# A gated delta rule whose scan applies raw keys and then the triangular inverse, in a two-layer hybrid trunk

## The chip, the cores and the metric

The kernel runs on one NeuronCore of one Trainium2 chip. The metric is the device time of an execution in microseconds (us). TensorE (PE) multiplies matrices into PSUM; VectorE (DVE), ScalarE (ACT) and GpSimd (POOL) work on SBUF tiles, and DVE and ACT read PSUM too; SyncE (SP) issues most of the DMA transfers. Each engine runs its own instructions in order and waits on semaphores for the others.

## What is computed

A trunk of two layers on 1024 tokens of width 1024: chunked attention with an MLP, then gated DeltaNet with an MLP, and a last norm. The change lies in DeltaNet, 8 heads of width 128. Per head, with queries `q` and keys `k` scaled to unit norm, `beta` a gate and `g` a log-decay, the reference does for chunks of 64 tokens:

```
gc = jnp.cumsum(g, axis=-1)
kb = k * beta[..., None];  vb = v * beta[..., None]
L = jnp.where(strict, jnp.einsum('bhnid,bhnjd->bhnij', kb, k) * decay, 0.0)
M = L + jnp.eye(CHUNK)
rhs = jnp.concatenate([vb, kb * jnp.exp(gc)[..., None]], axis=-1)
sol = lax.linalg.triangular_solve(M, rhs, left_side=True, lower=True, unit_diagonal=True)
u, w = sol[..., :dv], sol[..., dv:]
def step(state, inp):
    v_new = u_c - jnp.einsum('bhck,bhkv->bhcv', w_c, state)
    o_c = jnp.einsum('bhck,bhkv->bhcv', qd_c, state) + jnp.einsum('bhij,bhjv->bhiv', qk_c, v_new)
    state = state * gl_c[..., None, None] + jnp.einsum('bhck,bhcv->bhkv', kd_c, v_new)
    return state, o_c
```

`qk` holds the decayed products of queries and keys, `qd` the queries times exp(gc), `kd` the keys times exp(gc_last - gc), and `gl` the decay of a whole chunk. All is f32.

## The kernel before, in words

**Stages.** In the profiled execution attention takes until about 490 us, block 0 (output projection and MLP) until about 1198, DeltaNet until about 1804, and block 1 the rest. Dense products split each f32 operand into a high and a low part and take three products.

**DeltaNet's dense work.** `dn_run` (about L1835) goes through the projection's panels: keys of all heads, then queries, values and z (the output gate) of each head. A panel is 48 matmuls of 128x512: two halves of the tokens, eight slices of the width, three products. In the profile they are `acc<-xs,whi` and `acc<-xs,wlo`.

**What stands between.** After every dense matmul `dn_run` calls `turn`, which lets each task that is ready take a step. Tasks are generators with a priority from the table `G` (scans 0 and 0.1, solves 0.5, inverses 2, blocks 3, keys and values 4, queries 5, outputs 7, weights 8). A task waits for a mark of another one (`until`), for some planned time (`sleep`) or for a tile of a ring (`take`, `give`). A clock of planned costs decides what counts as ready. The order that comes of it is fixed when the program is built, for PE, DVE, ACT and POOL; SP's order is made by the framework's scheduler. Every operation of a task goes through one helper, so the profile shows it at line L163.

**The tasks of a head h.** The work is in blocks of 128 tokens, eight a head.

- `dn_inverses` (L2279 and on) builds the inverse of M for the eight blocks in the tile Zh, which starts at zero and of which there are two; head h waits for the values of head h-2.
- `dn_prep_keys` (L2374 to L2404): a DMA (L2379) loads the raw keys of the head into `kn`, width across partitions, 128 rows of 4 KB. PE transposes four blocks at a time into a PSUM tile (`tp<-ident,kn`), and DVE makes two scaled copies: `kbg` (beta, exp(gc) and the norm `rk`) and `kd`.
- `dn_prep_queries` (L2406 to L2445): `l2_sums` (L2155 to L2171) squares the queries qT on ACT into `nt` and sums over the width with eight one-column multiplies by ones on PE (`tp<-ones,nt`). The row of scales is broadcast by DMA (L1902), the decay `dc` loaded (L2412). PE forms qT·kn (`tp<-qT,kn`), DVE multiplies it by dc into `qk`, and POOL writes the scaled queries into the second half of `WQ`, a tile [128, 8, 2, 128] with two buffers.
- `dn_prep_values` (L2447 to L2488): transposes v, DVE scales it to `vb`; then, for each half of the blocks, PE forms Z·vb (`tp<-vb,Zh`) which ACT copies back to vb (this is u), and kbg·Z (`tp<-Zh,kbg`), which ACT copies into the first half of WQ (this is w).
- `dn_scans` (L2490 to L2535), two tasks, for even and odd heads. A step p multiplies the state by both halves of WQ (`s<-st,WQ`), DVE subtracts (vn = u - w·state), PE forms kd·vn and adds qk·vn to the output in PSUM, DVE updates the state (`st<-st,gl,s`), ACT copies the output block to `o`. The even heads' PSUM tiles appear as `s`, those of the odd heads as parts of `zz`.
- `dn_outs` squares, normalizes and gates o; `dn_reload` brings it back as the operand of the output projection.

Of the kernel before, what the change touches and what calls it, by code (L numbers as in the profile page):

```python
# [7 lines left out]
F32 = mybir.dt.float32  # L8
# [226 lines left out]
class Trunk:  # L235
# [1668 lines left out]
    def dn_gates(self):  # L1904
# [16 lines left out]
        for n in range(2):  # L1921
# [7 lines left out]
        yield  # L1929
        abd = self.abd  # L1930

        room = [self.whole(t).rearrange("p (n t) -> p n t", t=P) for t in ("kn", "qT")]
        used = []

        def t64(name):
# [219 lines left out]
    def l2_sums(self, x, scale, v):  # L2155

        nc = self.nc
        squares = yield from self.take("nt", 2)
        for h in range(2):
            nc.scalar.activation(squares[h], x[:, h * HB : (h + 1) * HB], AF.Square)  # L2160
            yield
        ps = yield from self.take("tp")
        for n in range(8):
            c = slice(n % 4 * P, (n % 4 + 1) * P)
            nc.tensor.matmul(ps[:, n : n + 1], squares[n // 4][:, c], self.ones, start=True, stop=True)
        self.give("nt", *squares)
        yield

        nc.vector.tensor_scalar(v, ps[:, :8], EPS, scale, ALU.add, ALU.mult)
        self.give("tp", ps)  # L2170
        yield  # L2171

    def rsqrt_few(self, v, n, who):
# [105 lines left out]
    def dn_inverse(self, h):  # L2279

        nc, db = self.nc, self.db
        Z = self.Zh[h % 2]
        X = self.X[:, :, 0:32]
        U12 = self.dq.tile([P, 8, 32], F32, name=self.nm("ua"), tag="ua")
        U34 = self.dq.tile([P, 8, 64], F32, name=self.nm("ub"), tag="ub")
# [8 lines left out]
            nc.gpsimd.tensor_tensor(U12[r], U12[r], wide(self.rk[r, h], 32, 32), ALU.mult)  # L2294
        nc.gpsimd.tensor_tensor(U34[0:64], U34[0:64], wide(self.rk[0:64, h], 64, 64), ALU.mult)
        yield from self.until("solve", h // 4)
        if h >= 2:
            yield from self.until("values", h - 2)
        zd, xd = self.solved[h // 4]
        for b in range(4):  # L2300
            r = slice(b * 32 + (h % 4) * 8, b * 32 + (h % 4) * 8 + 8)
# [72 lines left out]
    def dn_prep_keys(self):  # L2374

        nc, db, cols = self.nc, self.db, self.cols
        for h in range(8):
            kn = self.heads["kn", h] = self.whole("kn")
            nc.sync.dma_start(kn, self.kd[h])  # L2379
            self.mark("kn", h)  # L2380
            yield from self.until("rk", h // 4)
            ck = self.sm.tile([P, 2, 8], F32, name=self.nm("ck"), tag="ck")
            for n in range(2):
                nc.vector.tensor_tensor(ck[:, n], cols[:, 2 + n, h], self.rk[:, h], ALU.mult)
            if h == 0:
                yield from self.until("solve", 0)
            yield from self.sleep(G["sl_keys"])
            if h:
                yield from self.until("values", h - 1)
            if h >= 2:  # L2390
                yield from self.until("scan", h - 2)
            kbg = self.dq.tile([P, 8, P], F32, name=self.nm("kbg"), tag="kbg")
            kd = db.tile([P, 8, P], F32, name=self.nm("kd"), tag="kd")
            for q in range(2):
                s = slice(4 * q, 4 * q + 4)
                tp, ps = yield from self.to_tokens(kn, q)
                for n, dst in enumerate((kbg, kd)):
                    nc.vector.tensor_tensor(dst[:, s], ps, wide(ck[:, n, s], P, P), ALU.mult)
                    if n:
                        self.give("tp", tp)  # L2400
                    yield
            self.heads["kk", h] = kbg, kd
            self.mark("keys", h)
            yield from self.until("queries", h)  # L2404

    def dn_prep_queries(self):  # L2406
        nc, db = self.nc, self.db
        for h in range(8):
            yield from self.until("q", h)
            qT = self.heads.pop(("q", h))  # L2410
            dc = self.whole("dc").rearrange("p (q t) -> p q t", t=P)
            nc.sync.dma_start(dc, self.decay[h])  # L2412
            if h == 0:
                yield from self.until("u", 6)
# [10 lines left out]
            kn = self.heads["kn", h]  # L2425
            if h >= 2:
                yield from self.until("scan", h - 2)
            qk = self.qks[h % 2]
            for q in range(2):
                s = slice(4 * q, 4 * q + 4)  # L2430
                tp = yield from self.take("tp")
                ps = tp.rearrange("p (q t) -> p q t", t=P)
                for t in range(4):
                    c = slice((4 * q + t) * P, (4 * q + t + 1) * P)
                    nc.tensor.matmul(ps[:, t], kn[:, c], qT[:, c], start=True, stop=True)
# [4 lines left out]
            WQ = db.tile([P, 8, 2, P], F32, name=self.nm("WQ"), tag="WQ")  # L2440
            nc.gpsimd.tensor_tensor(
                WQ[:, :, 1], qT.rearrange("p (q t) -> p q t", t=P), row.rearrange("p (q t) -> p q t", t=P), ALU.mult)
            self.heads["qq", h] = WQ, qk
            self.mark("queries", h)
            self.mark("q", "used", h)  # L2445
            yield

    def dn_prep_values(self):
        nc, db = self.nc, self.db
        for h in range(8):  # L2450
            yield from self.until("v", h)
            cols = self.cols
            vT, Z = self.heads.pop(("v", h)), self.Zh[h % 2]
# [12 lines left out]
            kbg, kd = self.heads.pop(("kk", h))  # L2466
            WQ, qk = self.heads.pop(("qq", h))
            for q in range(2):
                s = slice(4 * q, 4 * q + 4)
                tp = yield from self.take("tp")  # L2470
                ps = tp.rearrange("p (q t) -> p q t", t=P)
                for t in range(4):
                    nc.tensor.matmul(ps[:, t], Z[:, 4 * q + t], vb[:, 4 * q + t], start=True, stop=True)
                yield
                nc.scalar.activation(vb[:, s], ps, AF.Copy)
                self.give("tp", tp)
                yield
                tp = yield from self.take("tp")
                ps = tp.rearrange("p (q t) -> p q t", t=P)
                for t in range(4):  # L2480
                    nc.tensor.matmul(ps[:, t], kbg[:, 4 * q + t], Z[:, 4 * q + t], start=True, stop=True)
                yield
                nc.scalar.activation(WQ[:, s, 0], ps, AF.Copy)
                self.give("tp", tp)
                yield
            self.heads[h] = vb, WQ, qk, kd
            self.mark("values", h)
            yield  # L2488

    def dn_scans(self, odd):  # L2490

        nc, db = self.nc, self.db
        for h in range(odd, 8, 2):
            yield from self.until("values", h)
            u, WQ, qk, kd = self.heads.pop(h)
            if h:
                yield from self.until(*(("solve", 1) if h == 1 else ("out", h - 2)))
            o = self.heads["o", h] = db.tile([P, 8, P], F32, name=self.nm("o"), tag="o")
            st = None
            for p in range(8):  # L2500
                vn = u[:, p]
                ps = yield from self.take("s1")
                if st is not None:
                    nc.tensor.matmul(ps[:, 0], WQ[:, p, 0], st, start=True, stop=True, skip_group_check=True)
# [6 lines left out]
                    yield  # L2511
                if p < 7:
# [199 lines left out]
```

## Time and profile before

| | |
|---|---|
| runs (3), median | 2531.4 us (2529.29 to 2532.87) |
| the profiled execution | 2528.32 us |
| its span in the trace | 2526.2 us |
| granted TensorE clock over the span | 0.992 |
| TensorE busy | 2446.5 us |
| VectorE, ScalarE, GpSimd busy | 1765.3, 1194.2, 1275.8 us |
| DMA over the span | 398.94 MB, mean 158 GB/s |

A line of a group reads: line, engine, operation, output tile <- input tiles, sizes, xcount | busy us, mean ns of one | idle time of the engine just before, and what ended it. An f32 multiply of 128x128 is executed in two passes and leaves two records; a transpose and a dense matmul of rounded operands leave one. In the timeline a row is: start, length, engine, line, operation, xcount, and in brackets the engine's idle time before it and what ended it. The length of a matmul is its way through the array, longer than the distance to the next.

### The profile page before, as it was taken

Reading aid. Unit: us, or ns where it says so; the run is one execution under the profiler, and the core shown is the slowest. Engines: PE = TensorE matmul, PEld = TensorE weight load, DVE = VectorE, ACT = ScalarE, POOL = GpSimd, SP = SyncE. Lnnn points to the kernel's source line nnn. Section 1 sums busy time; section 2 is a strip of 40 time slices with the busy share of each in tenths; the row PEclk is TensorE's granted clock in tenths of the full one; section 3 lists DMA queues with packets and bytes.
Section 4 is the critical chain, followed back from the end, with each engine's and each line's share of the span. In section 5 each row is a group of like instructions: output and inputs, shape, how many; then the busy total and the mean of one; then the engine's idle time right before and its main releaser. Section 6 shows DMA issues by size and latency. Waiting matters only on the chain.

```text
span 2526.2 us, 36563 instructions
## 1 busy us (share of the span) xinstructions
PE 2446.5 (97%) x12748; PEld 2041.2 (81%) x12748; DVE 1765.3 (70%) x3064; ACT 1194.2 (47%) x2217; POOL 1275.8 (51%) x1076
## 2 busy tenths in 40 slices
PE   8999999999999999998989999999999999999997
PEld 6888888787888887886767888888787888887886
DVE  6666556678777688888558755545678777678887
ACT  6666667535555533334565333333335555433323
POOL 2444445613765466666455434433415666566655
PEclk9999999999999999999999999999999999999998
DMA  4222223423555978653255222223424555977752
GB/s 162 69 64 71 79 76 108 161 100 141 205 202 219 327 241 283 222 195 110 106 171 166 66 87 68 97 63 121 131 81 162 208 212 206 348 238 251 247 170 83
DMA packets 192760, 398.94 MB, mean 158 GB/s; under 512 B 53232, under 2 KB 59696, under 8 KB 192576
## 3 DMA queue, kind: packets, MB, share of 16 engines
q1 hardware_dynamic: 172848, 351.50, 41.5%
q10 hardware_dynamic: 19728, 45.12, 4.7%
q8 instruction: 100, 1.64, 0.3%
q14 instruction: 84, 0.69, 0.1%
HBM read 257.43 MB, written 130.71 MB: 154 GB/s over the span
## 4 chain that ended last, share of the span: by engine, by line
PE 68%; DVE 6%; DMA 2%; issue 2%; ACT 2%; POOL 1%; SPq 0%; ACTq 0%; DVEq 0%; POOLq 0%
PE y L1040 26%; PE z L1040 12%; PE acc L163 11%; PE acc L1040 7%; PE tp L163 5%; PE acc L306 2%; PE acc L305 2%; PE acc L304 2%; PE s L163 1%; PE zz L163 1%; DVE x L1545 1%; DMA row<-grows 1%; DVE xs L421 0%; DVE cy L163 0%; DMA xs<-gt 0%
## 5 line engine op out<-in xcount | busy, mean ns | idle before, releaser
L163 PE MATMUL acc<-xs,whi 128*128 128x512 f32 x1744 | 606.9, 410 | 9.7 <-DVE xp L163 4.7
L163 PEld LDWEIGHTS acc<-xs,whi 128*128 128x128 f32 x1744 | 321.4, 190 | 61.8 <-ACT whi L163 4.9
L163 PE MATMUL acc<-xs,wlo 128*128 128x512 f32 x864 | 352.2, 408 | 1.7 <-POOL wlo L163 1.7
L1040 PE MATMUL y<-xs,whi 128*128 128x512 f32 x1008 | 311.7, 390 | 5.2 <-DVE x L1545 1.8
L163 POOL TENSOR_TENSOR wlo<-wraw,whi 128x512 fp32r<-128x512 f32 x126 | 167.0, 1326 | 204.1 <-ACT whi L163 170.5
L1055 POOL TENSOR_TENSOR s<-wraw 128x256 f32<-128x256 f32 (+1 forms) x93 | 90.4, 972 | 350.1 <-DVE a L1046 169.9
L1040 PEld LDWEIGHTS y<-xs,whi 128*128 128x128 f32 x1008 | 188.9, 188 | 47.1 <-DVE x L1545 2.6
L1046 DVE TENSOR_TENSOR wlo<-wraw,whi 128x512 fp32r<-128x512 f32 (+1 forms) x182 | 208.7, 1147 | 25.8 <-ACT whi L1049 24.7
L1049 ACT ACTIVATE whi<-wraw 128x512 fp32r<-128x512 f32 (+2 forms) x191 | 146.4, 766 | 119.8 <-PE y L1040 83.5
L1049 ACT ACTIVATE a<-s 128x256 fp32r<-128x256 f32 x122 | 63.8, 524 | 280.6 <-PE y L1040 142.3
L1040 PE MATMUL y<-xs,wlo 128*128 128x512 f32 x504 | 196.2, 389 | 0.0
L1040 PE MATMUL y<-xs,a 128*128 128x512 f32 x732 | 187.7, 392 | 6.7 <-DVE x L1545 6.7
L1545 DVE TENSOR_TENSOR x<-y,x 128x512 f32<-128x512 f32 x240 | 165.1, 688 | 34.9 <-PE y L1040 27.2
L163 PEld LDWEIGHTS acc<-xs,wlo 128*128 128x128 f32 x864 | 164.5, 190 | 25.9 <-POOL wlo L163 2.1
L1040 PEld LDWEIGHTS y<-xs,a 128*128 128x128 f32 x732 | 136.1, 188 | 40.1 <-DVE x L1545 10.3
L1040 PE MATMUL y<-xs,ahi 128*128 128x512 f32 x512 | 158.7, 391 | 7.7 <-ACT nt L1234 7.7
L1040 PE MATMUL acc<-xs,whi 128*128 128x512 f32 x528 | 162.9, 390 | 0.0
L163 POOL TENSOR_SCALAR pr<-pr,rs 128x640 f32<-128x640 f32 (+4 forms) x128 | 88.1, 692 | 129.3 <-DVE rs L163 98.2
L1040 PE MATMUL z<-xs,whi 128*128 128x512 f32 x480 | 147.8, 389 | 0.0
L1122 DVE TENSOR_TENSOR c<-c 128x512 fp32r<-128x512 f32 x112 | 119.4, 1073 | 30.8 <-POOL c L1052 28.4
L163 POOL TENSOR_TENSOR cy<-cy,cz 128x512 f32<-128x512 f32 x48 | 62.5, 1302 | 150.3 <-DVE cz L163 107.8
L163 DVE CUSTOM_DVE_ANT_0 pr<-sp,bias 128x640 f32<-128x640 f32 (+4 forms) x128 | 83.8, 655 | 63.9 <-PE sp L163 62.9
(370 smaller groups left out, 6097.5 us busy)
## 6 DMA issues: line engine op xcount, KB each, us to landing
xs<-gt SPq DMA_DIRECT2D x256, 256.0 KB, 4.9
gt<-c SPq DMA_DIRECT2D x112, 512.0 KB, 2.9
wraw<-in_w_up_dram SPq DMA_DIRECT2D x64, 512.0 KB, 3.9
wraw<-in_w_down_dram SPq DMA_DIRECT2D x64, 512.0 KB, 4.7
r<-gr SPq DMA_DIRECT2D x88, 256.0 KB, 3.5
wraw<-in_w_in_dram SPq DMA_DIRECT2D x32, 512.0 KB, 3.8
gr<-ssum ACTq DMA_DIRECT2D x62, 256.0 KB, 3.2
wraw<-in_w_qkv_dram SPq DMA_DIRECT2D x30, 512.0 KB, 3.4
```

Of the source, the lines that this page charges most:

```text
L163: return call(*args, **more)
L304: nc.tensor.matmul(ps, hi[:, k], xh, start=(k == 0), stop=False)
L305: nc.tensor.matmul(ps, hi[:, k], xl, start=False, stop=False)
L306: nc.tensor.matmul(ps, lo[:, k], xh, start=False, stop=(k == KT - 1))
L1040: nc.tensor.matmul(ps, w[:, k], x, start=bool(first and f), stop=bool(last and e), skip_group_check=True)
L1046: self.nc.vector.tensor_tensor(lo, src, hi.bitcast(F32), ALU.subtract)
L1049: self.nc.scalar.activation(hi, src, AF.Copy)
L1055: self.nc.gpsimd.tensor_tensor(out, x, y, ALU.add)
L1122: nc.vector.tensor_tensor(t[z][:, HB:].bitcast(F32R), t[z][:, HB:], t[z][:, :HB], ALU.subtract)
L1545: nc.vector.tensor_tensor(x, ps, x, ALU.add)
```

## The change

The scan no longer uses w = Z·kbg. It uses that u - w·state = Z·(beta v - beta exp(gc) k·state): a step multiplies the state by the raw keys, DVE forms r = bg * (k·state) + vb with bg = -beta exp(gc) rk, PE multiplies Z by r, ACT copies the product from PSUM to vn, and kd·vn and qk·vn follow as before. The raw keys are loaded by DMA straight into the first half of WQ, in pieces of 512 bytes; `kn` and `kbg` go. The PSUM tile s2 holds Z·r first and then kd·vn.

With that the waits change. Keys of head h (from 2 on) wait for the scan of head h-2, whose WQ buffer they take, and no longer for the values and queries of the head before; queries no longer wait for that scan themselves, but sleep as the keys do. Z is used to the scan's end, so there are three Zh tiles, and the inverse of head h (from 3 on) waits for the scan of head h-3.

The squares of the queries are summed from transposes: two groups of four transposes into PSUM, an ACT square from PSUM, and a DVE reduction along the tokens' rows in place of the one-column multiplies.

```diff
     def l2_sums(self, x, scale, v):
...
-        squares = yield from self.take("nt", 2)
-        for h in range(2):
-            nc.scalar.activation(squares[h], x[:, h * HB : (h + 1) * HB], AF.Square)
-            yield
-        ps = yield from self.take("tp")
-        for n in range(8):
-            c = slice(n % 4 * P, (n % 4 + 1) * P)
-            nc.tensor.matmul(ps[:, n : n + 1], squares[n // 4][:, c], self.ones, start=True, stop=True)
...
+        for q in range(2):
+            t = yield from self.take("nt")
+            tp, ps = yield from self.to_tokens(x, q)
+            sq = t.rearrange("p (q t) -> p q t", t=P)
+            nc.scalar.activation(sq, ps, AF.Square)
+            self.give("tp", tp)
+            yield
+            nc.vector.tensor_reduce(v[:, 4 * q : 4 * q + 4], sq, AX.X, ALU.add)
...
     def dn_inverse(self, h):
-        if h >= 2:
-            yield from self.until("values", h - 2)
+        if h >= 3:
+            yield from self.until("scan", h - 3)
...
     def dn_prep_keys(self):
         for h in range(8):
-            kn = self.heads["kn", h] = self.whole("kn")
-            nc.sync.dma_start(kn, self.kd[h])
+            if h < 2:
+                yield from self.until("u", 3 + 4 * h)
+            else:
+                yield from self.until("scan", h - 2)
+            WQ = self.heads["WQ", h] = db.tile([P, 8, 2, P], F32, name=self.nm("WQ"), tag="WQ")
+            nc.sync.dma_start(WQ[:, :, 0], self.kd[h].rearrange("p (q t) -> p q t", t=P))
...
-            if h:
-                yield from self.until("values", h - 1)
-            if h >= 2:
-                yield from self.until("scan", h - 2)
...
-            yield from self.until("queries", h)
...
     def dn_prep_values(self):
-                for t in range(4):
-                    nc.tensor.matmul(ps[:, t], Z[:, 4 * q + t], vb[:, 4 * q + t], start=True, stop=True)
-                yield
-                nc.scalar.activation(vb[:, s], ps, AF.Copy)
...
-                for t in range(4):
-                    nc.tensor.matmul(ps[:, t], kbg[:, 4 * q + t], Z[:, 4 * q + t], start=True, stop=True)
-                yield
-                nc.scalar.activation(WQ[:, s, 0], ps, AF.Copy)
...
     def dn_scans(self, odd):
-                    vn = db.tile([P, P], F32, name=self.nm("vn"), tag=f"vn{odd}")
-                    nc.vector.tensor_tensor(vn, u[:, p], ps[:, 0], ALU.subtract)
+                    r = db.tile([P, P], F32, name=self.nm("r"), tag=f"r{odd}")
+                    nc.vector.scalar_tensor_tensor(
+                        r, ps[:, 0], self.heads["bg"][:, h, p : p + 1], vb[:, p], ALU.mult, ALU.add)
                     yield
+                s2 = yield from self.take("s2")
+                nc.tensor.matmul(s2, Z[:, p], r, start=True, stop=True)
+                yield
+                vn = db.tile([P, P], F32, name=self.nm("vn"), tag=f"vn{odd}")
+                nc.scalar.activation(vn, s2, AF.Copy)
+                yield
                 if p < 7:
-                    s2 = yield from self.take("s2")
                     nc.tensor.matmul(s2, kd[:, p], vn, start=True, stop=True)
+                else:
+                    self.give("s2", s2)
```

How the order moves is seen at three places. The first is PE in a step of head 7's scan before (`acc<-xs` is dense work, `x2` two of them in a row; the state's multiply counts two multiplies, by keys or w and by queries):

```order
5899 L163 MATMUL s_3575_17440<-st_17432,WQ_17246 128x128 x2
5900 L163 MATMUL acc_17392<-xs_11821,whi_17205 128x512
5901 L163 MATMUL acc_17392<-xs_11821,wlo_17206 128x512
5902 L163 MATMUL acc_17392<-xs_11823,whi_17205 128x512
5903 L163 MATMUL s_3577_17450<-vn_17444,kd_16948 128x128
5904 L163 MATMUL s_3575_17440<-vn_17444,qk_12245 128x128
```

and a step of the same head now:

```order
5918 L163 MATMUL zz<-st_17406,WQ_16799 128x128 x2
5919 L163 MATMUL acc_17358<-xs_11823,whi_17189 128x512 x2
5920 L163 MATMUL acc_17358<-xs_11823,wlo_17190 128x512
5921 L163 MATMUL zz<-r_17417,Zh_12240 128x128
5922 L163 MATMUL acc_17358<-xs_11825,whi_17189 128x512 x2
5923 L163 MATMUL acc_17358<-xs_11825,wlo_17190 128x512
5924 L163 MATMUL acc_17429<-xs_11810,whi_17301 128x512
5925 L163 MATMUL zz<-vn_17426,kd_16823 128x128
5926 L163 MATMUL zz<-vn_17426,qk_12247 128x128
```

Three dense matmuls stood between the state's multiply and the use of vn; now three stand ahead of Z·r and four behind it.

The second place is PE around head 4's sums of squares, before:

```order
5346 L163 MATMUL acc_15683<-xs_11811,whi_15351 128x512 x2
5347 L163 MATMUL s_3253_15689<-vn_15679,kd_14956 128x128
5348 L163 MATMUL s_3248_15674<-vn_15679,qk_12245 128x128
5349 L163 MATMUL tp_15692<-ones,nt_15658 128x1 x4
5350 L163 MATMUL tp_15692<-ones,nt_15659 128x1 x4
5351 L163 MATMUL acc_15683<-xs_11811,wlo_15352 128x512
```

and now:

```order
5353 L163 MATMUL acc_15582<-xs_11824,wlo_15390 128x512
5354 L163 MATMUL acc_15656<-xs_11811,whi_15389 128x512
5355 L163 MATMUL tp_15667<-ident,qT_15593 128x128 x4
5356 L163 MATMUL acc_15656<-xs_11811,whi_15389 128x512
5357 L163 MATMUL zz<-vn_15651,kd_15097 128x128
5358 L163 MATMUL zz<-vn_15651,qk_12247 128x128
```

One group of eight one-column multiplies became two groups of four transposes, of which the second stands about 14 dense matmuls further on.

The third place is SyncE's queue where head 4's keys are loaded (L2379 and L2382 load keys, L1902 broadcasts a row, L2303 and L2301 move pieces of the inverse, L1806 loads weights, L2412 the decay), before:

```order
655 L2288 DMA ub_15211<-u_12236 64x512
656 L1902 DMA row_15655<-grows 128x1024
657 L2379 DMA kn_15298<-kd 128x1024
658 L1806 DMA wraw_15428<-in_w_in_dram 128x1024
659 L2412 DMA dc_15653<-decay 128x1024
```

and now:

```order
650 L1806 DMA wraw_15491<-in_w_in_dram 128x1024
651 L1902 DMA row_15663<-grows 128x1024
652 L2303 DMA X<-xd_14554 32x8x32 x2
653 L2382 DMA WQ_15315<-kd 128x8x128
654 L2286 DMA ub_15296<-u_12236 64x512
655 L2301 DMA Zh_12242<-zd_14553 32x8x32 x4
656 L2412 DMA dc_15661<-decay 128x1024
```

The load of the keys now stands behind two small loads of X besides the row, and its target is a buffer that the scan of head 2 has to leave first.

More of the change, by code (lines that the diff above doesn't have):

```diff
@@ L1920, in dn_gates @@
         self.Zh = []
-        for n in range(2):
+        for n in range(3):
             z = d1.tile([P, 8, P], F32, name=f"Zh{n}")
@@ L1930, in dn_gates @@
         abd = self.abd
-        room = [self.whole(t).rearrange("p (n t) -> p n t", t=P) for t in ("kn", "qT")]
+        room = [self.whole(t).rearrange("p (n t) -> p n t", t=P) for t in ("kbg", "qT")]
         used = []
@@ L2157, in l2_sums @@
         nc = self.nc
-        squares = yield from self.take("nt", 2)
-        for h in range(2):
-            nc.scalar.activation(squares[h], x[:, h * HB : (h + 1) * HB], AF.Square)
-            yield
-        ps = yield from self.take("tp")
-        for n in range(8):
-            c = slice(n % 4 * P, (n % 4 + 1) * P)
-            nc.tensor.matmul(ps[:, n : n + 1], squares[n // 4][:, c], self.ones, start=True, stop=True)
-        self.give("nt", *squares)
-        yield
-        nc.vector.tensor_scalar(v, ps[:, :8], EPS, scale, ALU.add, ALU.mult)
-        self.give("tp", ps)
+        for q in range(2):
[4 more added lines that the diff above has]
+            self.give("tp", tp)
+            yield
+            nc.vector.tensor_reduce(v[:, 4 * q : 4 * q + 4], sq, AX.X, ALU.add)
+            self.give("nt", t)
+            yield
+        nc.vector.tensor_scalar(v, v, EPS, scale, ALU.add, ALU.mult)
         yield
@@ L2281, in dn_inverse @@
         nc, db = self.nc, self.db
-        Z = self.Zh[h % 2]
+        Z = self.Zh[h % 3]
         X = self.X[:, :, 0:32]
@@ L2376, in dn_prep_keys @@
         nc, db, cols = self.nc, self.db, self.cols
+        self.heads["bg"] = self.d1.tile([P, 8, 8], F32, name="bg")
         for h in range(8):
-            kn = self.heads["kn", h] = self.whole("kn")
-            nc.sync.dma_start(kn, self.kd[h])
+            if h < 2:
[4 more added lines that the diff above has]
+            nc.sync.dma_start(WQ[:, :, 0], self.kd[h].rearrange("p (q t) -> p q t", t=P))
             self.mark("kn", h)
             yield from self.until("rk", h // 4)
-            ck = self.sm.tile([P, 2, 8], F32, name=self.nm("ck"), tag="ck")
-            for n in range(2):
-                nc.vector.tensor_tensor(ck[:, n], cols[:, 2 + n, h], self.rk[:, h], ALU.mult)
+            ck = self.sm.tile([P, 2, 8], F32, name=self.nm("ck"), tag="ck")[:, 0]
+            nc.vector.tensor_tensor(ck, cols[:, 3, h], self.rk[:, h], ALU.mult)
+            nc.vector.scalar_tensor_tensor(
+                self.heads["bg"][:, h], cols[:, 2, h], -1.0, self.rk[:, h], ALU.mult, ALU.mult)
             if h == 0:
@@ L2387, in dn_prep_keys @@
             yield from self.sleep(G["sl_keys"])
-            if h:
-                yield from self.until("values", h - 1)
-            if h >= 2:
-                yield from self.until("scan", h - 2)
-            kbg = self.dq.tile([P, 8, P], F32, name=self.nm("kbg"), tag="kbg")
             kd = db.tile([P, 8, P], F32, name=self.nm("kd"), tag="kd")
@@ L2395, in dn_prep_keys @@
                 s = slice(4 * q, 4 * q + 4)
[L2396 to L2400, printed above, removed]
-                    yield
-            self.heads["kk", h] = kbg, kd
+                tp = yield from self.take("tp")
+                ps = tp.rearrange("p (q t) -> p q t", t=P)
+                for t in range(4):
+                    nc.tensor.transpose(ps[:, t], WQ[:, 4 * q + t, 0], self.ident)
+                yield
+                nc.vector.tensor_tensor(kd[:, s], ps, wide(ck[:, s], P, P), ALU.mult)
+                self.give("tp", tp)
+                yield
+            self.heads["kk", h] = kd
             self.mark("keys", h)
-            yield from self.until("queries", h)
     def dn_prep_queries(self):
@@ L2424, in dn_prep_queries @@
             yield from self.until("kn", h)
-            kn = self.heads["kn", h]
-            if h >= 2:
-                yield from self.until("scan", h - 2)
+            yield from self.sleep(G["sl_keys"])
+            WQ = self.heads["WQ", h]
             qk = self.qks[h % 2]
@@ L2434, in dn_prep_queries @@
                     c = slice((4 * q + t) * P, (4 * q + t + 1) * P)
-                    nc.tensor.matmul(ps[:, t], kn[:, c], qT[:, c], start=True, stop=True)
+                    nc.tensor.matmul(ps[:, t], WQ[:, 4 * q + t, 0], qT[:, c], start=True, stop=True)
                 yield
@@ L2452, in dn_prep_values @@
             cols = self.cols
-            vT, Z = self.heads.pop(("v", h)), self.Zh[h % 2]
+            vT, Z = self.heads.pop(("v", h)), self.Zh[h % 3]
             if h >= 2:
@@ L2465, in dn_prep_values @@
                 yield from self.until(key, h)
-            kbg, kd = self.heads.pop(("kk", h))
+            kd = self.heads.pop(("kk", h))
             WQ, qk = self.heads.pop(("qq", h))
[L2468 to L2471, printed above, removed]
-                for t in range(4):
-                    nc.tensor.matmul(ps[:, t], Z[:, 4 * q + t], vb[:, 4 * q + t], start=True, stop=True)
-                yield
-                nc.scalar.activation(vb[:, s], ps, AF.Copy)
[L2476 to L2479, printed above, removed]
-                for t in range(4):
-                    nc.tensor.matmul(ps[:, t], kbg[:, 4 * q + t], Z[:, 4 * q + t], start=True, stop=True)
-                yield
-                nc.scalar.activation(WQ[:, s, 0], ps, AF.Copy)
-                self.give("tp", tp)
-                yield
-            self.heads[h] = vb, WQ, qk, kd
+            self.heads[h] = vb, WQ, qk, kd, Z
             self.mark("values", h)
@@ L2494, in dn_scans @@
             yield from self.until("values", h)
-            u, WQ, qk, kd = self.heads.pop(h)
+            vb, WQ, qk, kd, Z = self.heads.pop(h)
             if h:
@@ L2500, in dn_scans @@
             for p in range(8):
-                vn = u[:, p]
+                r = vb[:, p]
                 ps = yield from self.take("s1")
@@ L2508, in dn_scans @@
                     yield
-                    vn = db.tile([P, P], F32, name=self.nm("vn"), tag=f"vn{odd}")
-                    nc.vector.tensor_tensor(vn, u[:, p], ps[:, 0], ALU.subtract)
+                    r = db.tile([P, P], F32, name=self.nm("r"), tag=f"r{odd}")
+                    nc.vector.scalar_tensor_tensor(
+                        r, ps[:, 0], self.heads["bg"][:, h, p : p + 1], vb[:, p], ALU.mult, ALU.add)
                     yield
+                s2 = yield from self.take("s2")
+                nc.tensor.matmul(s2, Z[:, p], r, start=True, stop=True)
+                yield
+                vn = db.tile([P, P], F32, name=self.nm("vn"), tag=f"vn{odd}")
+                nc.scalar.activation(vn, s2, AF.Copy)
+                yield
                 if p < 7:
-                    s2 = yield from self.take("s2")
                     nc.tensor.matmul(s2, kd[:, p], vn, start=True, stop=True)
+                else:
+                    self.give("s2", s2)
                 ready = self.clock.end
```

1 line of the change is left out of this document (removed).

## The prediction

> **What bounds the kernel now.** I read the page first, then busy time by stretch, the chain of waits, the groups by form, and the timeline where instructions change. The page gives span and TensorE share; the stretches (columns: start:end, length, then busy time of PE, PEld, DVE, ACT and POOL, then granted clock, DMA share, GB/s) are DeltaNet's front, its body and its tail.
>
> ```profile
> span 2526.2 us, 36563 instructions
> PE 2446.5 (97%) x12748; PEld 2041.2 (81%) x12748; DVE 1765.3 (70%) x3064; ACT 1194.2 (47%) x2217; POOL 1275.8 (51%) x1076
> 1198.00:1360.00 162.00, 140.00 (x674) 114.42 (x674) 104.95 (x219) 94.94 (x170) 77.68 (x64) 0.96 0.44 140
> 1360.00:1784.00 424.00, 422.46 (x3110) 361.55 (x3109) 242.50 (x559) 161.47 (x317) 161.36 (x120) 0.99 0.29 92
> 1784.00:1804.20 20.20, 15.12 (x48) 10.18 (x48) 12.76 (x23) 8.57 (x16) 9.85 (x8) 0.75 0.51 161
> ```
>
> The change touches only DeltaNet, and nearly all of it lies in the body, where PE is busy 422.5 of 424 us. The chain of waits there (shares of the chain from 1360 to 1780) and the one wait of PE say the same:
>
> ```profile
> by line: PE acc L163 57.6%; PE tp L163 26.2%; PE s L163 7.1%; PE zz L163 5.1%; issue 1.8%; DVE cy L163 0.9%; POOL wlo L163 0.3%; DVE ru L163 0.3%; POOL ua L163 0.3%; POOL ub L163 0.2%; DVE xs L163 0.2%; DVE cz L163 0.2%; DVE st L163 0.1%; D
> PE s L163 <- DVE ft L163: 1.5, 1, 1.5
> ```
>
> So 96% of the chain is PE's own work and PE waited once, 1.5 us. Here a microsecond of PE work taken away is a microsecond, as long as no new wait appears; DVE (57% busy), ACT (38%) and POOL (38%) gain nothing by losing work.
>
> **What a multiply costs.** The groups' busy time is a union, with overlaps given to one side, so I take start-to-start times where a group stands between dense matmuls. First the groups from 1195 to 1850 (an f32 multiply leaves two records, so x128 is 64 multiplies; a transpose leaves one):
>
> ```profile
> L163 PE MATMUL tp<-Zh,kbg 128*128 128x128 f32 x128 | 17.1, 276 | 0.0
> L163 PE MATMUL tp<-ones,nt 128*128 128x1 f32 x128 | 15.3, 248 | 1.9 <-ACT nt L163 1.9
> L163 PE MATMUL tp<-ident,kn 128*128 128x128 f32 x64 | 9.8, 275 | 0.0
> ```
>
> Then PE's timeline (start, length, operation) around a kbg·Z group, a transpose group and a one-column group:
>
> ```profile
> 1699.74 0.39 PE L163 MATMUL acc<-xs,whi 128*128 128x512 f32 x1
> 1699.97 1.05 PE L163 MATMUL tp<-Zh,kbg 128*128 128x128 f32 x8
> 1700.78 0.48 PE L163 MATMUL acc<-xs,whi 128*128 128x512 f32 x1
> 1701.09 0.40 PE L163 MATMUL acc<-xs,wlo 128*128 128x512 f32 x1
> ...
> 1702.24 0.60 PE L163 MATMUL tp<-ident,o 128*128 128x128 f32 x4
> 1702.59 0.48 PE L163 MATMUL acc<-xs,whi 128*128 128x512 f32 x1
> 1702.91 1.05 PE L163 MATMUL tp<-vb,Zh 128*128 128x128 f32 x8
> ...
> 1509.32 1.84 PE L163 MATMUL tp<-ones,nt 128*128 128x1 f32 x16
> 1511.02 0.48 PE L163 MATMUL acc<-xs,whi 128*128 128x512 f32 x1
> 1511.33 0.61 PE L163 MATMUL s<-st,WQ 128*128 128x128 f32 x4
> ```
>
> A dense matmul takes 0.23 (1699.74 to 1699.97). Four kbg·Z multiplies and one dense matmul take 1701.09 - 1699.97 = 1.12, so one multiply takes (1.12 - 0.23) / 4 = 0.22. Four transposes and one dense matmul take 1702.91 - 1702.24 = 0.67, so one takes 0.11. Eight one-column multiplies and one dense matmul take 2.01, so one takes 0.22: a column costs as much as 128.
>
> **The change, part by part.**
>
> *kbg·Z goes* (8 heads x 8 = 64 multiplies): 64 x 0.224 = -14.3 us; by the group's row -17.1 at most.
>
> *Z·vb becomes Z·r in the scan*: 64 multiplies go, 64 come, same shape, all still in the body: 0.
>
> *Queries' squares*: 64 one-column multiplies (64 x 0.224 = 14.3) become 64 transposes (64 x 0.109 = 7.0): -7.3. The rows allow -5.5 (15.3 - 9.8). PE's sum is so -21.6.
>
> *ACT, DVE, POOL off the path*: ACT loses 32 copies of 128x512 and gains 64 of 128x128, DVE loses kbg's products (16) and gains reductions (16); one more memset on POOL comes ahead of the matmuls that could wait for it. The body's cover is ACT 262 and DVE 181 us idle. 0. In the front DVE is nearly full around head 0's queries, and two reductions of 0.68 are new there; against them stands PE's wait of 1.9 us for nt, which has no successor, since a transpose reads qT, an operand that is there earlier. I take 0, bounds -1.9 to +1.4.
>
> *A longer chain in the scan.* A step was PE (W·state), DVE (subtract), PE (k·v, qk·v), DVE (state); it becomes PE, DVE, PE (Z·r), ACT (copy), PE, DVE. What decides is whether the dense matmuls between cover each hop. PE's and DVE's timeline of a step of head 7, and the groups of the engines' small operations:
>
> ```profile
> 1758.26 0.60 PE L163 MATMUL s<-st,WQ 128*128 128x128 f32 x4
> 1759.41 0.38 PE L163 MATMUL s<-vn,kd 128*128 128x128 f32 x2
> 1759.63 0.39 PE L163 MATMUL s<-vn,qk 128*128 128x128 f32 x2
> 1758.91 0.29 DVE L163 TENSOR_TENSOR vn<-vb,s 128x128 f32<-128x128 f32 x1 [0.25 <-PE s L163]
> L163 DVE TENSOR_TENSOR vn<-vb,s 128x128 f32<-128x128 f32 x35 | 10.0, 285 | 16.8 <-PE s L163 16.8
> L163 DVE SCALAR_TENSOR_TENSOR st<-st,gl,s 128x128 f32<-128x128 f32 x27 | 9.3, 345 | 13.1 <-PE s L163 12.9
> L163 ACT ACTIVATE o<-s 128x128 f32<-128x128 f32 x36 | 10.0, 277 | 53.4 <-PE s L163 48.6 <-DVE st L163 1.8 <-DVE ru L163 1.0
> L163 ACT ACTIVATE nt<-qT 128x512 f32<-128x512 f32 x16 | 9.8, 620 | 0.0
> ```
>
> The old hop: start of W·state to end of the subtract 1759.20 - 1758.26 = 0.94, the next PE use at 1759.41, margin 0.21, and it made no stall. The new DVE operation has the form of st (0.345 for 0.285): margin 0.15, still cover. The new hop: in the order four dense matmuls lie between Z·r and k·v, so PE asks 0.22 + 4 x 0.23 = 1.15 after Z·r starts; the result needs the multiply's latency (estimate 0.43: W·state's four records reach DVE 0.65 after their start, 1758.26 to 1758.91, and two records less are 0.22 less) plus ACT's copy (0.28) = 0.70, margin 0.4. An ACT operation of 0.62 that has just begun would eat it and leave about 0.2. ACT is busy 38% of the time; if a quarter of the 64 copies meets such an operation late enough to cost 0.1, it is 16 x 0.1 = 1.6. I take +1.5; the bounds are 0 (the order is arranged for it) and 64 x 0.62 = 40 (each copy behind a whole operation). I stay near the low end because the old hop with a smaller margin never stalled.
>
> *Keys arrive later.* Raw keys went early into a buffer of their own; now they go into the scan's WQ buffer, which head h-2 must have finished. The DMA rows of 1230 to 1800 (KB each, median us to landing) and SyncE's wait ahead of a row broadcast (total, times, longest):
>
> ```profile
> kn<-kd SPq DMA_DIRECT2D x8, 512.0 KB, 5.1
> dc<-decay SPq DMA_DIRECT2D x8, 512.0 KB, 6.0
> x<-xd SPq DMA_DIRECT2D x8, 512.0 KB, 7.1
> SPq L1902 <- POOL WQ L163: 34.8, 4, 12.0
> ```
>
> For heads 2 to 7 the order leaves 21 to 23 dense matmuls and six to twelve small operations between the last use of the old buffer and the first of the new: about 6.2 to 6.9 us (21 x 0.23 + 6 x 0.22 = 6.2). The load needs 5.1 as it is; in pieces of 512 bytes instead of 4 KB I expect it nearer to the slower loads of that size on the same queue (6.0 and 7.1 in the other rows), and take 5.6. With the hand-over that is cover, with margins of some tenths. I put 0.3 on each of five heads, +1.5. Head 4's load alone stands on SyncE behind a row broadcast, which waits for POOL's product into WQ, up to 12.0 in the row, and behind two small loads: I expect it 2 to 4 late, +3. Bounds: 0, and 6 x 3 = 18.
>
> The Trainium skill ("DMA: Bandwidth & Descriptors", Specifications) puts the smallest transfer at line rate at 512 bytes; by it the finer pieces would cost nothing, and the five heads' 1.5 would be about 0. No run here yet shows a 512 KB load in such pieces.
>
> *Tail.* Scan 7 ends some 10 to 30 dense matmuls later, but the wait at the end is for reload and normalization of o, not for the scan: 0, bounds -1 to +4.
>
> *The clock.* Idle PE is followed by half clock, and so is one long one-column group (second row, 0.83 in the 10 us behind it):
>
> ```profile
> 1311.23 1.19 PE L163 MATMUL acc<-xs,whi 128*128 128x512 f32 x2 [4.69 <-DVE xp L163]
> 1510.00:1520.00 10.00, 10.00 (x69) 9.01 (x68) 2.34 (x9) 1.85 (x5) 2.66 (x4) 0.83 0.06 16
> ```
>
> At 0.83, 1.7 us of work are lost once in the body; transposes come in two separate groups of four and replace that group, so this may go: 0 to -1.7, I take 0.
>
> A rule speaks the other way: the Trainium skill ("TensorE: Matmul & The Clock Gate", Part 4) says that a transpose does not count as busy for the clock gate, so more transposes would mean more half clock. If it held at groups of 0.44 us among dense matmuls, the existing transposes (192 and more in the body) should show it; the granted clock of the body is 0.99, so the trace does not bear it out at this spacing.
>
> **Sum:** -21.6 + 1.5 + 1.5 + 3 + 0 = -15.6. The profiled execution took 2528.3 (its span 2526.2), so 2512.7; the median of the runs before is 2531.4, and 15.6 less is 2515.8. I predict 2516.
>
> **The rivals.**
>
> *The whole saving arrives* (0.17): keys land in time, ACT keeps up, and the half clock goes: -21.6 to -25, about 2508. For it: no stall in 424 us says the order leaves room. Against: the tight key loads.
>
> *Keys late at each head* (0.15): each of six loads 1.5 to 3 late, +9 to +18, so -4 to -13, about 2523. For it: SyncE's queue waits a lot (34.8 us on one line); against: cover of 6.2 for a load of 5.1.
>
> *ACT's queue holds the scan* (0.08): the copy of vn stands in order behind operations that wait for DVE or POOL themselves. With 0.5 us lost at each of 64 steps it is +32 against -21.6: +10, 2542, slower. It decides from 21.6 / 64 = 0.34 us per step; a dense matmul more than the margin of 0.4. Against it: ACT is idle 62% of the body and o's copies already follow the same multiplies.
>
> *Hardly any change* (0.05): lost and saved time cancel within 5 us, for instance a longer tail (+4) on top of late keys.
>
> A measurement of this kernel tells 0.2%, about 5 us, from no change. The forecast (-10 to -21) has 0.55. The range: 2506 (all the saving and one half clock) to 2527 (keys late everywhere), leaving 0.08 + 0.05 and some low tail outside. Faster: 0.55 + 0.17 + 0.14 of the late keys' 0.15 = 0.86; same: 0.05, 0.01 of the late keys and 0.01 of ACT's = 0.07; slower: 0.07.
>
> **What would show it.** Right: PE's records from 1360 on are as dense as before and the body is 17 to 22 us shorter; no tp<-Zh,kbg and no tp<-ones,nt; a wait of PE for DMA WQ at head 4 of 2 to 4 us and little elsewhere. Wrong: PE waiting for ACT vn in many steps (ACT rival), or for WQ at each head (keys), or granted clock below 0.97 in the body (transposes), or a stretch from the last z matmul to block 1 that is over 24 us (tail).

## The result and the profile after

The changed kernel takes 2505.43 us (median of 4 runs, 2504.68 to 2507.67), the kernel before 2530.48 beside it (2529.29 to 2532.87): 25.0 us less, a ratio of 0.9906 with a 95% interval from 0.9894 to 0.9918. The forecast was 2516; its sign held and so did PE's sum, its centre was 10.6 us too careful, and the time lies 0.6 us under the range (2506 to 2527).

The page of the kernel after, span and engines:

```profile
span 2502.9 us, 36230 instructions
PE 2423.3 (97%) x12556; PEld 2014.0 (80%) x12556; DVE 1771.2 (71%) x3064; ACT 1192.5 (48%) x2249; POOL 1280.1 (51%) x1077
```

TensorE's busy time fell by 23.2 us, the span by 23.3. To see where, the same piece of dense work is compared: from dense matmul 492 of the stage to 1532, counted in the records of both traces. First before, then after (columns as in the prediction):

```profile
1361.50:1778.73 417.23, 415.69 (x3081) 356.03 (x3080) 237.30 (x544) 159.42 (x314) 157.66 (x117) 1.00 0.29 91
```

```profile
1358.30:1752.50 394.20, 392.27 (x2877) 329.34 (x2876) 239.03 (x547) 154.99 (x341) 159.96 (x118) 1.00 0.29 90
```

The body is 23.0 us shorter and as dense as before: PE idle 1.5 us then, 1.9 now. The work explains it. 64 products kbg·Z went (14.3). Seven groups of eight one-column multiplies (12.5) became 15 groups of four transposes (6.5; head 0's first group lies ahead of the stretch). Twelve multiplies of the last scan steps (24 records, 2.7) moved behind its end. That is 23.0; the half clock behind the group at 1509 is gone too (1.7), and 0.4 of waits came: 24.3 by the price of 0.224 a multiply, 22.5 by the 0.21 that `more_pe` gives below, for the 23.0 measured.

Just ahead of it, from dense matmul 372 to 492, PE is 3.8 us quicker, around head 0's queries. PE's timeline there before the change (start, length, operation, idle time before it and what ended it), and the granted clock (0.66) behind the second group:

```profile
1355.42 1.05 PE L163 MATMUL tp<-ones,nt 128*128 128x1 f32 x8 [0.35 <-ACT nt L163]
1358.05 1.31 PE L163 MATMUL tp<-ones,nt 128*128 128x1 f32 x8 [1.57 <-ACT nt L163]
1358.00:1363.00 5.00, 4.95 (x19) 4.19 (x20) 4.12 (x13) 1.69 (x3) 3.30 (x3) 0.66 0.69 139
```

The timeline after the change:

```profile
1353.96 0.63 PE L163 MATMUL tp<-ident,qT 128*128 128x128 f32 x4 [1.14 <-DVE U L163]
...
1359.01 0.60 PE L163 MATMUL tp<-ident,qT 128*128 128x128 f32 x4
1359.37 0.71 PE L163 MATMUL acc<-xs,whi 128*128 128x512 f32 x2
```

The two waits for nt and the half clock after the second are not there; a new wait of 1.14 for U is. All waits of PE between these two matmuls add to 4.4 before and 3.4 after (1.0 less), the half clock cost about 1.5 (0.96 over these 39.5 us, 1.00 after), and eight one-column multiplies (1.8) became four transposes (0.4).

In the tail, from matmul 1532 to the first product of block 1, 0.6 us are given back (25.5 before, 26.1 after), although the twelve multiplies (2.7) moved there and PE's wait for o grew from 1.9 to 2.9. The granted clock is higher: 0.75 before (the prediction's row from 1784), 0.92 after:

```profile
1760.00:1782.00 22.00, 17.37 (x70) 12.86 (x70) 14.01 (x24) 8.77 (x18) 10.24 (x7) 0.92 0.75 258
```

From matmul 372 to block 1 the stage is so 26.3 us shorter. The span is only 23.3 shorter, because of stretches that do not show the change: the profiled execution reached DeltaNet 3.2 us later than that of before, was 2.5 quicker up to matmul 372 (shorter waits for wlo, xp and ft; in the experiments' traces the same stretch is 0.7 to 3.6 us longer than here), and lost 2.3 in block 1.

PE's waits in the stage from 1323 to 1757 show what the longer chain costs, and the groups what it is made of:

```profile
PE tp L163 <- DVE U L163: 1.9, 2, 1.1
PE acc L163 <- POOL wlo L163: 1.5, 1, 1.5
PE tp L163 <- ACT nt L163: 0.5, 1, 0.5
PE tp L163 <- DVE vb L163: 0.4, 1, 0.4
PE tp L163 <- issue: 0.4, 1, 0.4
PE s L163 <- ACT vn L163: 0.3, 1, 0.3
PE tp L163 <- DMA X<-xd: 0.2, 1, 0.2
```

```profile
L163 PE MATMUL s<-r,Zh 128*128 128x128 f32 x68 | 13.3, 276 | 0.0
L163 PE MATMUL zz<-r,Zh 128*128 128x128 f32 x44 | 8.7, 280 | 0.0
L163 PE MATMUL tp<-ident,qT 128*128 128x128 f32 x64 | 9.6, 273 | 1.1 <-DVE U L163 1.1
L163 ACT ACTIVATE vn<-s 128x128 f32<-128x128 f32 x36 | 9.9, 275 | 27.0 <-PE s L163 26.8
L163 DVE SCALAR_TENSOR_TENSOR r<-s,bg,vb 128x128 f32<-128x128 f32 x35 | 12.2, 349 | 20.4 <-PE s L163 20.0
```

No wait for WQ stands in the list at all, and vn is waited for once, 0.3 us (once more behind it, 0.4 at the scans' last step). ACT's copy is 0.28 and DVE's new form 0.35, as priced. Z·r behaves as the products it replaces.

### The profile page after: what moved, and what is told of

It is laid out like the page before. It is cut to its first block, busy times and chain, and to the rows that moved or that the text cites. A ratio compares the mean times of both kernels' runs of the same rounds, so it can differ in the third digit from the quotient of the medians.

```text
span 2502.9 us, 36230 instructions
## 1 busy us (share of the span) xinstructions
PE 2423.3 (97%) x12556; PEld 2014.0 (80%) x12556; DVE 1771.2 (71%) x3064; ACT 1192.5 (48%) x2249; POOL 1280.1 (51%) x1077
## 4 chain that ended last, share of the span: by engine, by line
PE 66%; DVE 7%; DMA 3%; ACT 2%; issue 2%; SPq 1%; POOL 0%; ACTq 0%; DVEq 0%; POOLq 0%
PE y L1040 26%; PE z L1040 12%; PE acc L163 10%; PE acc L1040 7%; PE tp L163 3%; PE zz L163 2%; PE acc L306 2%; PE acc L304 2%; PE acc L305 2%; PE s L163 1%; DVE x L1545 1%; DMA wraw<-in_w_up_dram 1%; DVE xs L421 0%; DVE cz L163 0%; DMA xd<-x 0%
## 5 line engine op out<-in xcount | busy, mean ns | idle before, releaser
L1046 DVE TENSOR_TENSOR wlo<-wraw,whi 128x512 fp32r<-128x512 f32 (+1 forms) x182 | 209.6, 1152 | 26.3 <-ACT whi L1049 26.3
```

Of the source, the lines that this page charges most:

```text
L1046: self.nc.vector.tensor_tensor(lo, src, hi.bitcast(F32), ALU.subtract)
```

## The experiments

Theory: the gain is PE's own work taken out of a saturated body, plus what PE lost around the one-column groups; the longer scan chain and the late key loads are covered. Rivals: the gain comes of looser coupling and not of the multiplies; or chain and loads already cost something that the sum hides. Differences from the changed kernel are between medians (2505.4); each kernel was also timed beside the kernel before. By the intervals, such a difference is uncertain by some 3 to 4 us; taken by way of the kernels before (2529.0 to 2531.2), the differences would shift by up to 1.5.

**The two halves alone.** `l2_only` is the kernel before with the new `l2_sums`; `scan_only` is the changed kernel with the old one, the same lines the other way round.

```diff
-            nc.scalar.activation(squares[h], x[:, h * HB : (h + 1) * HB], AF.Square)
...
-            nc.tensor.matmul(ps[:, n : n + 1], squares[n // 4][:, c], self.ones, start=True, stop=True)
+            tp, ps = yield from self.to_tokens(x, q)
+            sq = t.rearrange("p (q t) -> p q t", t=P)
+            nc.scalar.activation(sq, ps, AF.Square)
...
+            nc.vector.tensor_reduce(v[:, 4 * q : 4 * q + 4], sq, AX.X, ALU.add)
```

> The kernel before with the squares summed from transposes, and W formed as before. Theory (the gain is PE's work, plus what PE lost at the one-column groups): -7.3 us of multiplies, -1.9 of wait for nt and -1.7 of half clock at head 0, perhaps -1.7 of the half clock at 1512: 9 to 13 us under the kernel before, no half clock from 1323 to the tail. Rival (only the multiplies' price counts, the waits and the half clock move elsewhere): 5 to 8 under it.

Measured: 2523.4 against 2531.2, ratio 0.9975 (0.9966 to 0.9984), 7.8 us: the rival's number. The wait for nt is gone, but new waits came: in that plan PE waits for wlo, for X and for vn at places of their own, and behind the wait for X there is half clock (0.69 from 1380 to 1385), which the theory had excluded.

```profile
PE acc L163 <- POOL wlo L163: 2.6, 1, 2.6
PE tp L163 <- DVE U L163: 2.0, 2, 1.2
PE tp L163 <- DMA X<-xd: 1.9, 1, 1.9
PE zz L163 <- DVE vn L163: 1.4, 1, 1.4
```

> The changed kernel with the squares summed by one-column multiplies as before: only W is gone. Theory: -14.3 us of multiplies, up to 1.5 of a wait, against the kernel before: 13 to 17 under it, half clock and a wait for nt around head 0's one-column groups again. Rival (the scan's new form gains more than its multiplies, because the tasks are coupled less): 20 or more under it.

Measured: 2517.0 against 2531.2, ratio 0.9941 (0.9927 to 0.9955), 14.3 us: the price of the 64 multiplies, with no sign of a looser coupling, though its five runs lie from 2511.0 to 2517.9. The wait for nt is back with its 1.9 us, and half clock behind it (0.56 from 1358 to 1363):

```profile
PE tp L163 <- ACT nt L163: 1.9, 2, 1.6
```

The halves add to 22.1, the whole is 25.0; the 3 us between them are within the uncertainty, and single waits fall elsewhere in each plan.

**The form of the sum.** One-column multiplies in two groups of four, in the changed kernel:

```diff
+            ps = yield from self.take("tp")
+            for n in range(4):
+                nc.tensor.matmul(ps[:, n : n + 1], sq[:, n * P : (n + 1) * P], self.ones, start=True, stop=True)
```

> The changed kernel with one-column multiplies in two separate groups of four, where it has transposes. Theory (a one-column multiply costs 0.224, a transpose 0.109, the half clock comes of the long group of eight): 7.3 us over the changed kernel, granted clock 1.00 in the body. Rival (one-column multiplies bring half clock however they are grouped): 9 to 11 over it, with stretches of half clock.

Measured: 2516.5 against 2531.2, 0.9938 (0.9926 to 0.9951): 11.0 over the changed kernel, the rival's size, and stretches of half clock are there (0.73 from 1380 to 1385). But their cause is not shown to be the form: PE waits for ACT nt again (2.1), and for others, and that stretch of half clock begins behind the wait of 1.2 for cy at 1380.7.

```profile
PE tp L163 <- ACT nt L163: 2.1, 1, 2.1
PE acc L163 <- POOL wlo L163: 1.7, 1, 1.7
PE tp L163 <- DVE cy L163: 1.2, 1, 1.2
PE tp L163 <- DMA WQ<-kd: 1.0, 1, 1.0
```

So head 0 was tried apart from heads 1 to 7, with old and new `l2_sums` side by side:

```diff
-            yield from self.l2_sums(qT, 128.0 * EPS, v)
+            yield from (self.l2_ones if h == 0 else self.l2_sums)(qT, 128.0 * EPS, v)
```

> The changed kernel with the squares of head 0 alone summed by one-column multiplies, those of heads 1 to 7 from transposes. Theory (at head 0 PE, which is not saturated there yet, waits for ACT's squares and then runs 3.4 us at half clock): 0.9 us of multiplies, 1.9 of wait and 1.7 of half clock, 3 to 5 us over the changed kernel. Rival (only the multiplies' price counts): 0 to 2 over it.

Measured: 2509.3 against 2529.2, 0.9920 (0.9907 to 0.9934): 3.9 over the changed kernel for one head, where the multiplies are 0.9. PE's timeline has the two waits, and the stretch behind them the half clock (0.72 over 6 us is 1.7):

```profile
1355.05 1.05 PE L163 MATMUL tp<-ones,nt 128*128 128x1 f32 x8 [0.37 <-ACT nt L163]
1357.66 1.05 PE L163 MATMUL tp<-ones,nt 128*128 128x1 f32 x8 [1.56 <-ACT nt L163]
```

```profile
1358.00:1364.00 6.00, 6.00 (x24) 4.91 (x24) 5.76 (x16) 3.92 (x7) 4.38 (x3) 0.72 0.70 197
```

The 3.9 is not the price of head 0 alone, though. This plan also has waits that the changed kernel has shorter or not at all, one of 5.1 for ft at 1319.5 (1.5 there) and one of 2.8 for r at 1444.7 with a second stretch of half clock behind it (0.67 from 1445 to 1450), and it lacks others, such as the 1.5 for wlo. That the total meets the expectation is in part luck. What does hold in every trace is the pair: with the waits for nt at head 0 (before, `scan_only`, `ones_in_fours`, `ones_head_0`) the granted clock from 1358 to 1363 is 0.56 to 0.66; no trace without them has half clock there.

> The other way round: head 0 from transposes, heads 1 to 7 by one-column multiplies in groups of eight. Theory: 7 x 8 x 0.115 = 6.4 us of multiplies over the changed kernel, no wait for nt at head 0, so 5 to 8 over it. Rival (what the one-column form costs beyond its multiplies is spread over all heads): 9 or more over it.

The same edit with `h > 0`. Measured: 2510.3 against 2529.2, 0.9922 (0.9908 to 0.9935): 4.9 over, the multiplies of seven heads (6.4) within the uncertainty. So at heads 1 to 7 the new sums gain roughly what the multiplies cost; how much head 0 brings beyond its own is not settled by these two runs, whose plans differ in other waits.

**Is the body PE's work?** Each product of queries and keys is issued twice into the same place; the rows of all engines stay in their order:

```diff
                     nc.tensor.matmul(ps[:, t], WQ[:, 4 * q + t, 0], qT[:, c], start=True, stop=True)
+                    nc.tensor.real.matmul(ps[:, t], WQ[:, 4 * q + t, 0], qT[:, c], start=True, stop=True)
```

> The changed kernel with each of the 64 multiplies of queries and keys issued twice into the same place, in the same order on every engine: 64 more f32 multiplies in the body. Theory (the body is PE's own work throughout): 64 x 0.224 = 14.3 us over the changed kernel. Rival (PE has slack behind other engines in places, or a repeated multiply is cheaper): under 10 over it.

Measured: 2518.8 against 2531.2, 0.9952 (0.9940 to 0.9965): 13.4 over the changed kernel for 64 multiplies, 0.21 each. The price that the timeline gave (0.224) holds within the uncertainty, and the body alone, between the same dense matmuls as above, is 13.2 longer.

**The margin of the scan's new hop.** One and two more copies of vn onto itself behind the first, PE's order unchanged:

```diff
                 nc.scalar.activation(vn, s2, AF.Copy)
+                nc.scalar.real.activation(vn, vn, AF.Copy)
```

> The changed kernel with one more 128x128 ACT copy (vn onto itself) in each of the 64 scan steps, between Z times r and its use; the order on PE is the same. Theory (the hop PE, ACT, PE has about 0.4 us of margin at a step): the extra copy of 0.28 is covered nearly everywhere, 0 to 3 us over the changed kernel. Rival (the hop is tight and every delay reaches PE): 64 x 0.28 = 18 us over it.

Measured: 2507.8 against 2529.0, 0.9915 (0.9902 to 0.9929): 2.4 over. Its four runs are 2505.5 twice and 2510 to 2511 twice; the profiled one, of the longer two, has a wait of 1.3 for r with half clock behind it (0.89 and 0.77 from 1395 to 1405), so the added copy itself is covered, as far as these runs tell.

> The same with two more copies, 0.56 us a step. Theory of a margin of 0.4: 0.1 to 0.2 us late at each step, 6 to 13 us over the changed kernel, with PE waiting for ACT vn in most steps. Rival (tight): 36 over it. Rival (margin of a microsecond): under 2.

Measured: 2522.5 against 2529.0, 0.9973 (0.9963 to 0.9984): 17.1 over, 0.27 a step. A step of it near 1753, PE and then ACT:

```profile
1752.42 0.38 PE L163 MATMUL s<-r,Zh 128*128 128x128 f32 x2
1752.56 0.48 PE L163 MATMUL acc<-xs,wlo 128*128 128x512 f32 x1
1752.87 0.63 PE L163 MATMUL acc<-xs,whi 128*128 128x512 f32 x2
1753.34 0.39 PE L163 MATMUL acc<-xs,wlo 128*128 128x512 f32 x1
1753.86 0.49 PE L163 MATMUL s<-vn,kd 128*128 128x128 f32 x2
```

```profile
1752.84 0.28 ACT L163 ACTIVATE vn<-s 128x128 f32<-128x128 f32 x1 [1.63 <-PE s L163]
1753.15 0.31 ACT L2498 ACTIVATE vn<-vn 128x128 f32<-128x128 f32 x1
1753.49 0.31 ACT L2499 ACTIVATE vn<-vn 128x128 f32<-128x128 f32 x1
```

ACT begins 0.42 after Z·r does and ends its third copy at 1753.80; kd·vn starts at 1753.86, where the dense work alone would have let it start at 1753.57. Each added copy takes 0.33 with its hand-over (1753.15 to 1753.49 and on), so two take 0.65, PE is 0.29 late, and the margin is 0.36. The forecast had 0.4 from the rows of before. In the changed kernel itself that margin is left over: the term of +1.5 was too high.

**The engine of the copy.**

```diff
-                nc.scalar.activation(vn, s2, AF.Copy)
+                nc.vector.tensor_copy(vn, s2)
```

> The changed kernel with DVE making vn's copy from PSUM in place of ACT, with the order planned anew. Theory (neither engine's hop reaches PE): within 3 us of the changed kernel. Rival (ACT's queue costs the scan something that the sum hides): 3 or more under it.

Measured: 2518.3 against 2529.0, 0.9957 (0.9944 to 0.9969): 12.8 over the changed kernel; both lines of the expectation missed. PE waits for DVE. In the changed kernel's body DVE is busy 61% and ACT 39% of the time, here 64% and 35%, and DVE's queue holds three operations of each step:

```profile
PE s L163 <- DVE vn L163: 4.9, 4, 2.5
PE tp L163 <- DVE o L163: 2.9, 1, 2.9
PE s L163 <- DVE r L163: 2.6, 3, 1.2
PE tp L163 <- DVE U L163: 1.9, 2, 1.1
PE zz L163 <- DVE r L163: 1.7, 2, 1.2
```

The order was planned anew, so the 12.8 is the price of the copy on DVE together with the order that comes of it.

**The margin of the key loads.** Each head's keys are loaded into WQ twice:

```diff
             nc.sync.dma_start(WQ[:, :, 0], self.kd[h].rearrange("p (q t) -> p q t", t=P))
+            nc.sync.dma_start(WQ[:, :, 0], self.kd[h].rearrange("p (q t) -> p q t", t=P))
```

> The changed kernel with each head's keys loaded into WQ twice, the second load behind the first; the order on PE is the same. The first load lands 4.2 us after its issue (median), the cover is about 6.2. Theory (the loads are just covered): if the second waits for the first, landing comes about 8.5 us after the issue, 2 to 3 us late at heads 2 to 7: 10 to 18 us over the changed kernel, with PE waiting for DMA WQ. If the two overlap, 0 to 4 over it. Rival (the loads have far more cover than 6.2 us): under 2 over it although the second lands at 8 or later.

Measured: 2532.2 against 2529.0, 1.0013 (1.0003 to 1.0023): 26.8 over the changed kernel, more than the theory gave. The eleven runs lie from 2528.5 to 2541.7, and the profiled one is the longest, 37 over the changed kernel's profiled run; what follows explains that one. PE's wait at six heads, and one of them, at head 5, on SyncE and PE:

```profile
PE tp L163 <- DMA WQ<-kd: 13.6, 6, 2.9
```

```profile
1579.85 0.54 SPq L2382 DMA_DIRECT2D WQ<-kd  x1
1584.04 0.52 SPq L2383 DMA_DIRECT2D WQ<-kd  x1
```

```profile
1588.19 0.63 PE L163 MATMUL tp<-ident,WQ 128*128 128x128 f32 x4 [2.16 <-DMA WQ<-kd]
```

The second load follows the first by 4.2 us, and lands 2.2 us late, as the theory had it. The rest is the clock: the 10 us behind that wait have half of it, though PE is busy throughout.

```profile
1580.00:1590.00 10.00, 7.84 (x41) 6.00 (x39) 3.82 (x8) 2.88 (x7) 6.09 (x4) 0.95 0.70 220
1590.00:1600.00 10.00, 10.00 (x97) 7.95 (x97) 2.29 (x5) 1.57 (x4) 0.00 (x0) 0.50 0.05 11
```

Not every wait has this behind it. Of the six, two are followed by a long stretch (0.51 from 1589 to 1603, 0.54 from 1650 to 1665), one by a short one (0.66 from 1537 to 1542) and three by none; a wait of 2.8 for X at 1380, not for keys, has a long one too (0.54 from 1380 to 1395). The four stretches lose 22 us by these clocks; with the waits of 13.6 and 2.8 that is 39, for the 37 measured.

In the changed kernel the single load at the same place was issued at 1560.42 and its keys used at 1566.43: 6.0 us of cover for a load of 4.2 (below), 1.8 to spare. By `keys_twice`, without that cover the change would lose what it wins.

## Why the prediction was right, and where its size was off

- **PE's sum (-21.6)** held: 14.3 for W by `scan_only` and 0.21 a multiply by `more_pe`; the body's own balance gives 23.0, less the 2.7 that moved into the tail, plus 1.4 for head 0's group ahead of it: 21.7. Shown for W and for the price; for the queries' squares `ones_heads_1_7` (4.9 for 6.4) and `l2_only` (7.8) agree within their uncertainty. The body was to be 17 to 22 us shorter; it is 23.0.
- **A longer chain in the scan (+1.5)**: the margin was read rightly (0.4, measured 0.36), its price not. The prediction let a quarter of the copies meet an operation of ACT that eats the margin; PE's waits for vn are 0.3 us in the body. About 0.3 stands in its place.
- **Keys arrive later (+1.5 and +3)**: this step failed most, 4.5 of the 10.6, and the wait of 2 to 4 us for WQ at head 4, named as a sign of being right, is not there. The load in pieces of 512 bytes takes 4.2 (median), not 5.6. The load of dc, whole rows, whose 6.0 the 5.6 leaned on, takes 3.6 after the change:

```profile
WQ<-kd SPq DMA_DIRECT2D x8, 512.0 KB, 4.2
dc<-decay SPq DMA_DIRECT2D x8, 512.0 KB, 3.6
```

 So the landing times of before did not carry over to the new order, even for a load that kept its form; why they are shorter is open.

 Head 4's load, expected 2 to 4 late behind the row broadcast, was issued at 1513.64, 1.4 us behind the broadcast (1512.24), and its keys used at 1519.31: 5.7 of cover. The wait of 12.0 that I had quoted belonged to the order before; SyncE's row for the same wait is now at most 3.8:

```profile
SPq L1902 <- POOL WQ L163: 14.1, 6, 3.8
```

 The Trainium skill ("DMA: Bandwidth & Descriptors", Specifications) puts the smallest transfer at line rate at 512 bytes; by it the finer pieces cost nothing. The 4.2 does not contradict it, but no run here separates the size of the pieces from the rest of the traffic.
- **Head 0's queries and the clock (0 and 0)**: the bound was right (-1.9 for the wait), the value taken was not. The wait went, less a new one (1.0 in all), and so did a half clock behind it (about 1.5), which stood in no term of the sum. The half clock at 1512 was absent after (1.7), but that the one-column form causes it is not shown: groups of eight brought none in the body of `scan_only` from 1370 on and one in that of `ones_heads_1_7` (0.80 and 0.86 from 1435 to 1445), and `copy_1_more`, with transposes alone, has one too, behind its wait for r.
- **The tail (0)**: 0.6 back. That it is near 0 is luck: 2.7 of moved work and 1.0 of a longer wait for o stand against a higher clock, none of which the prediction weighed.
- **The rule on transposes and the clock gate** (the Trainium skill, "TensorE: Matmul & The Clock Gate", Part 4): some 60 more transposes in the body, on top of 184 before, left its granted clock at 1.00 (the two rows of the body in the section on the result), so at groups of four among dense matmuls it did not show.

The rival "the whole saving arrives", at 0.17 and 2508, is what happened. The terms that I added against it, 6 us in all, and some 4 us left at zero (the wait at head 0 and the two half clocks) make up the 10. The other rivals were real mechanisms without effect here: a late copy costs what its margin says once it is used up (`copy_2_more`), and late keys cost their wait and, in part, half clock behind it (`keys_twice`).

What stays open: why the clock stays low for 10 us and more after a wait of 2.2 in `keys_twice`, not at all after others of its length, and for only 3.4 after the 4.7 us wait before the change; the long stretch holds many 32x32 multiplies and transposes, but no run separates that. What brings the half clock at 1512 before the change is open too.

## What to carry to other kernels

In a stage where one engine is busy 99% of the time, price the change by the start-to-start time of that engine's instructions, and then check each new hop and load for its margin in units of the work that lies between, from the order; here every term with a positive margin came to about zero. Take a load's landing time as a range, since it moves with the order: dc's went from 6.0 to 3.6. A wait that disappears can take the slow clock behind it along: at head 0 about 1.5 us of it on top of the wait. Which engine makes a copy in a chain matters by what else its queue holds: a copy of 0.28 us made PE wait 0.3 us in the body on ACT, and the kernel planned with it on DVE took 12.8 us longer.

## What the runs showed of the hardware

- A multiply with one column costs PE as much as one with 128 (0.22 for f32), a transpose half of it (0.11).
- 512 KB from HBM into 1024 pieces of 512 bytes landed in 4.2 us (median of 8). Whole rows of 4 KB landed in 5.1 (kn) and 6.0 (dc) before the change, and in 3.6 (dc) after it on the same queue.
- A late operand of 2.2 us was followed by 10 us at half clock with PE busy throughout; of six such waits in the run (13.6 us) three had half clock behind them and three had none.
- In the clock records of all twelve traces, every stretch of half clock within DeltaNet lasts 3.4 us or two, three or four times that.
